# Gated MLP layer on one core: u and gate of 1088 tokens as seven products of halves, on quarters of 272 columns

## The chip, the core and the metric

The kernel runs on one core of a Trainium2 chip. Its metric is the device time of one execution in microseconds (us); three runs of the kernel before gave a median of 946.48 (944.19 to 948.4). The engines are TensorE (PE in the profile; PEld is its weight load), VectorE (DVE), ScalarE (ACT), GpSimd (POOL) and SyncE (SP), which issues all of the DMAs here. Each has its own queue of instructions.

## The reference

Two layers on 1088 tokens (1024 of a prompt, 64 of a sample), width 1024: a gated linear attention and a chunked MLP that mixes tokens, each with RMSNorm ahead and a residual; then a last RMSNorm. The change is in the second layer:

```python
def cmlp_mixer(h, w_in, ln_g, ln_b, w_spatial, b_spatial, w_out):
    u, v, gate = jnp.split(h @ w_in, 3, axis=-1)
    v = layernorm(v, ln_g, ln_b)
    ...
    mixed = jnp.einsum('gts,bnsgd->bntgd', ws, vg) + bs.T[:, :, None]
    z = u * mixed.reshape(bsz, t, CMLP_WIDTH) * jax.nn.silu(gate)
    return z @ w_out, v
```

## The kernel before

Activations lie in SBUF with 128 features on the partitions, 8 feature tiles `kt`, and tokens along the free axis. Tokens come in three pieces of 384, 384 and 320 (`PIECES`), each with an activation tile of its own (`act_slot`). Every float32 operand is split into a high and a low part in fp32r (ACT copies the high part, DVE subtracts it for the low part), and every product is three passes: high by high, high by low, low by high.

The second layer has three stages. The **v stage** (blocks 16 to 19 of the weights, nine chunks of 128 tokens each, the last 64) computes v by token and stores it to DRAM; beside it, `token_sums` builds sums of activations. The **u/gate loop** then goes over the eight column blocks `m` of 128. The **output products** (blocks 28 to 31) follow. From the v stage to the end of the loop every engine's instructions keep the order in which the code writes them (`in_order`).

In block `m`, u and gate of tokens 0 to 767 are one product of 2 x 2 quarters: the weights by (even or odd feature tile, u or gate), the activations by (even or odd feature tile, first or second 384 tokens). It takes seven products instead of eight (`product`, L987 to L990, 12 matmuls of 384 columns each). Four of them use sums of weight quarters, `s1` to `s4`; four use sums of activations, `tsum` 0 to 3. The sample and the rest of the prompt, 320 tokens, are done by plain products (`u` and `gate`, 24 matmuls of 320 columns each).

What sets the order of work in a block:

- `raw_quarters` (L937 to L940): SP loads the raw weights of a block, four DMAs of 256 KB, into one tile `rawq`. There is one such tile, so the next load waits for the last reader of the one before.
- `Quarters.sums` (L958, POOL): `s1` to `s4` from `rawq`. `Quarters.parts` and `plain` (`parts_of`, L943 to L946): high part on ACT, low part on DVE, of a sum or of a plain quarter such as (1,2).
- `v_load`, `v_norm`, `mixed` (L1062, L1072, L1088 to L1096): v of 128 columns comes from DRAM into `vm`, ACT normalizes it (nine steps), TensorE mixes it over tokens, DVE writes the result to `zt`. `v_out` (L1080, L1081, POOL) makes the output rows in `bc`.
- L1152 to L1154 and L1162 (POOL), L1141, L1161, L1169, L1170 (DVE): the seven products are joined into gate (`sg`) and u. `rs` is the norm's factor of each token. L1171 (ACT) is Silu, L1178 and L1184 (DVE) multiply the gate into `zt`, which is stored to DRAM. `pb`, `pe`, `p1` and `p6` are partial results; `pb` and `pe` are banks in PSUM that hold one product and then take another one on top.
- `late` (L1207 on) ends the plain part of a block inside the next block, and there issues the load of the weights for the block after that.

Of the kernel before, what the change touches and what calls it, by code (L numbers as in the profile page):

```python
# [28 lines left out]
NPMAX = 384  # L29

# [8 lines left out]
def trunk_kernel(ctx: ExitStack, tc: tile.TileContext, a: dict):  # L39
# [57 lines left out]
    rs = [cp.tile([P, n], F32, tag=f"rs{p}", name=f"rs{p}") for p, n in enumerate(size)]  # L97
# [88 lines left out]
    def act_slot(p, name):  # L186
        return ap_.tile([P, 2, KT, size[p]], F32R, tag=f"act{p}", name=name)
# [685 lines left out]
    kp = pool("sums23")  # L873
# [27 lines left out]
    tsum = [(kp if i in (1, 2) else mp).tile([P, 2, 4, NPMAX], F32R, tag=f"tsum{i}", name=f"tsum{i}") for i in range(4)]  # L901
# [6 lines left out]
    def split_to(dst, k, src):  # L908
        A.activation(dst[:, 0, k, :], src, AF.Copy)
        V.tensor_tensor(dst[:, 1, k, :], src, dst[:, 0, k, :].bitcast(F32), ALU.subtract)  # L910

    def token_sums(k):

        x = vp.tile([P, 2, 2, NPMAX], F32, tag="xsum", name="xsum")
        for p in range(2):
            SP.dma_start(x[:, p], a["x1_spill"][:, 2 * k:2 * k + 2, NPMAX * p:NPMAX * p + NPMAX])
# [32 lines left out]
    class Quarters:  # L949
        def __init__(self, blk):  # L950
# [3 lines left out]
            self.w = {}  # L954
# [19 lines left out]

    def quarter(p, e):
        return [(h1[p][:, 0, 2 * k + e, :], h1[p][:, 1, 2 * k + e, :]) for k in range(4)]

    class Halves:

        def __init__(self, *tiles):  # L980
            self.tiles = tiles

        def __getitem__(self, i):
            return self.tiles[i[2] // 4][i[0], i[1], i[2] % 4, i[3]]
# [9 lines left out]
    steps = (s for k in range(4) for s in token_sums(k))  # L994
    nxt = None
    for blk in range(16, 20):
        cs = slice((blk - 16) * 256, (blk - 15) * 256)
        for i in range(9):
            t = vp.tile([P, 256], F32, tag="vt", bufs=4, name="vt")
            if i < 8:  # L1000
                A.activation(t, tm_block(ws_[blk], h1[i // 3], (i % 3) * P), AF.Copy)  # L1001
# [8 lines left out]
            if blk < 19:  # L1010
                if i in (0, 1, 2):
                    load_w(blk + 1, i)
                if i in (2, 3, 4, 5):
                    fetch_w(blk + 1, [i - 2])
                    if i == 2:
                        load_w(blk + 1, 3)
            if (blk, i) == (16, 3):
                held.pop()(2)
            if blk == 17 and i in (2, 5, 8):
                token_rstd(i // 3)  # L1020
            if (blk, i) >= (16, 4):
                next(steps, None)
            if (blk, i) == (18, 4):
                nxt = Quarters(20)
            if blk == 19:
                if i == 0:
                    nxt.sums("s1")
                elif i == 1:
                    nxt.sums("s2")
                elif i == 2:  # L1030
                    nxt.sums("s3")
                    nxt.parts("s1")
                elif i == 3:
# [20 lines left out]
    nxt.plain((1, 1))  # L1054
# [5 lines left out]
    def v_load(m):  # L1060

        t = up.tile([P, 9, P], F32, tag="vm", bufs=2, name="vm")  # L1062
# [21 lines left out]
    def mixed(dst, vm, g, m, bias, c0, nch, sample):  # L1084

        pm = ps("o", "mix")
        for c in range(nch):
            PE.matmul(pm[:, c * P:(c + 1) * P], vm[:, c0 + c, :], ws[:, g, :], start=True, stop=True)  # L1088
        n = nch * P
        if sample:  # L1090
            PE.matmul(pm[:, n:n + NS], vm[:, 8, :], wss[:, g, :], start=True, stop=True)
        V.scalar_tensor_tensor(dst[:, :n].rearrange("p (c t) -> p c t", c=nch),
                               pm[:, :n].rearrange("p (c t) -> p c t", c=nch), lng[:, m:m + 1],
                               over(bias, nch), ALU.mult, ALU.add)
        if sample:
            V.scalar_tensor_tensor(dst[:, n:n + NS].rearrange("p (b t) -> p b t", b=NB),  # L1096
                                   pm[:, n:n + NS].rearrange("p (b t) -> p b t", b=NB), lng[:, m:m + 1],
                                   over(bias[:, :8], NB), ALU.mult, ALU.add)
# [273 lines left out]
```

## Time and profile before

| What | Value |
|---|---|
| Median of three runs | 946.48 us |
| The profiled execution, its own time | 945.69 us |
| Its span, first to last instruction | 943.9 us |
| Mean granted TensorE clock | 0.995 |
| Instructions | 16451 |
| HBM over the span | 103 GB/s |

The profile is of one execution. Busy time of an engine is the time in which an instruction of it runs; waits and DMA issues are not counted. Matmuls are pipelined, so one's duration overlaps the next. An idle time is put down to the instruction or transfer that ended last before it. Names such as L958 are lines of the kernel; `a<-b` reads "writes a, reads b".

### The profile page before, as it was taken

What the parts mean: (1) busy time and instruction counts of PE and PEld (TensorE: products, weight loads), DVE (VectorE), ACT (ScalarE), POOL (GpSimd) and SP (SyncE); (2) the same over time, 40 slices, a digit from 0 to 9 for tenths busy, and PEclk for the clock granted to TensorE, in tenths of its full rate; (3) what the DMA queues carried; (4) which work ended last, traced back from release to release, by engine and by line L of the source; (5) the groups of instructions that cost most, each with busy time, mean ns of one, the idle gap of its engine ahead of it and who ended that gap; (6) DMA issues with size and microseconds to landing.
All of it is one profiled execution on the core that took longest, in us unless ns stands there. A gap on an engine that the chain in (4) does not pass through costs nothing.

```text
span 943.9 us, 16451 instructions
## 1 busy us (share of the span) xinstructions
PE 909.9 (96%) x6149; PEld 884.2 (94%) x6149; DVE 624.3 (66%) x1239; ACT 447.0 (47%) x940; POOL 305.6 (32%) x315
## 2 busy tenths in 40 slices
PE   9989999999999999989999999999899999989995
PEld 8979989998999899978999999999899999989994
DVE  7888778677885877688552944455666666773246
ACT  7664544454462555464342733336444444454322
POOL 2023332333322331322143121144655555302123
PEclk9999999999999999999999999999999999999998
DMA  9302113311232112324574143523333333384233
GB/s 296 95 1 82 50 36 87 110 38 36 67 103 60 63 41 84 103 83 126 154 255 141 62 152 121 177 73 100 97 97 97 97 97 97 116 259 123 58 109 129
DMA packets 89644, 98.40 MB, mean 104 GB/s; under 512 B 9927, under 2 KB 82061, under 8 KB 89565
## 3 DMA queue, kind: packets, MB, share of 16 engines
q1 hardware_dynamic: 89564, 97.36, 33.6%
q8 instruction: 48, 0.79, 0.3%
q14 instruction: 32, 0.25, 0.1%
HBM read 70.92 MB, written 26.42 MB: 103 GB/s over the span
## 4 chain that ended last, share of the span: by engine, by line
PE 66%; DVE 15%; ACT 6%; issue 6%; DMA 5%; POOL 2%; SPq 1%; DVEq 0%; ACTq 0%; POOLq 0%
PE fm L132 26%; PE tm L146 15%; PE pb L990 4%; PE p L990 3%; PE pe L990 3%; PE u L990 2%; PE gate L990 2%; PE sc L508 2%; PE tms L162 1%; DVE wq L946 1%; PE pst L579 1%; PE mix L1088 1%; DMA xsum<-x_spill 1%; PE o L618 1%; DVE scT L521 1%
## 5 line engine op out<-in xcount | busy, mean ns | idle before, releaser
L146 PE MATMUL tm<-w,h 128*128 128x256 f32 (+1 forms) x1536 | 192.7, 283 | 1.6 <-ACT vt L1001 1.2
L132 PE MATMUL fm<-h,w 128*128 128x384 f32 (+1 forms) x1056 | 188.7, 333 | 0.1
L146 PEld LDWEIGHTS tm<-w,h 128*128 128x128 f32 x1536 | 185.4, 188 | 3.4 <-ACT vt L1001 1.6
L132 PEld LDWEIGHTS fm<-h,w 128*128 128x128 f32 x1056 | 174.4, 188 | 2.0 <-DVE h L196 0.7
L132 PE MATMUL fm<-og,w 128*128 128x384 f32 (+1 forms) x576 | 102.0, 332 | 0.4 <-DVE og L193 0.4
L132 PEld LDWEIGHTS fm<-og,w 128*128 128x128 f32 x576 | 95.1, 188 | 1.6 <-DVE og L193 0.6
L118 DVE TENSOR_TENSOR w<-wr,w 128x512 fp32r<-128x512 f32 (+1 forms) x96 | 71.3, 758 | 21.4 <-ACT w L117 20.6
L117 ACT ACTIVATE w<-wr 128x512 fp32r<-128x512 f32 (+1 forms) x96 | 58.6, 624 | 26.6 <-DMA wr<-w 14.5
L132 PE MATMUL fm<-zs,w 128*128 128x384 f32 (+1 forms) x384 | 64.0, 326 | 1.4 <-DVE x L838 1.4
L816 POOL TENSOR_TENSOR acc<-acc,sq 128x384 f32<-128x384 f32 (+1 forms) x30 | 30.9, 1034 | 105.6 <-ACT sq L811 105.1
L132 PEld LDWEIGHTS fm<-zs,w 128*128 128x128 f32 x384 | 62.3, 188 | 2.6 <-DVE x L838 2.0
L838 DVE TENSOR_TENSOR x<-fm,res 128x384 f32<-128x384 f32 (+1 forms) x40 | 21.0, 527 | 54.5 <-PE fm L132 54.5
L811 ACT ACTIVATE sq<-x 128x384 f32<-128x384 f32 (+1 forms) x42 | 21.0, 503 | 62.2 <-DVE x L838 59.4
L1008 DVE BATCH_NORM_STATS2 st<-vt 128x6 f32<-128x256 f32 (+1 forms) x36 | 15.2, 421 | 42.4 <-ACT vt L1001 42.2
L463 POOL TENSOR_TENSOR xe<-xe,k 128x384 f32<-128x384 f32 (+2 forms) x24 | 28.5, 1187 | 45.2 <-ACT xe L462 42.0
L649 POOL TENSOR_TENSOR on<-on,g 128x384 f32<-128x384 f32 (+1 forms) x24 | 23.8, 1013 | 57.0 <-DVE on L648 34.6
L439 POOL TENSOR_TENSOR kd<-kd,k 128x384 f32<-128x384 f32 (+1 forms) x12 | 12.0, 1004 | 85.8 <-ACT kd L438 85.8
L990 PE MATMUL pb<-tsum,wq 128*128 128x384 f32 x192 | 37.2, 341 | 2.5 <-DVE wq L946 1.4
L990 PEld LDWEIGHTS pb<-tsum,wq 128*128 128x128 f32 x192 | 33.7, 188 | 3.7 <-DVE wq L946 1.8
L990 PE MATMUL p<-h,wq 128*128 128x384 f32 x192 | 36.4, 337 | 0.0
L990 PE MATMUL pe<-tsum,wq 128*128 128x384 f32 x192 | 36.2, 336 | 0.0
L132 PE MATMUL fm<-tsum,w 128*128 128x384 f32 x192 | 34.3, 338 | 1.6 <-DVE z L1199 1.6
(271 smaller groups left out, 1855.2 us busy)
## 6 DMA issues: line engine op xcount, KB each, us to landing
wr<-w SPq DMA_DIRECT2D x92, 256.0 KB, 3.1
rawq<-w SPq DMA_DIRECT2D x32, 256.0 KB, 3.5
s<-s SPq DMA_DIRECT2D x16, 256.0 KB, 5.9
state_s<-ns SPq DMA_DIRECT2D x32, 128.0 KB, 2.5
v_spill<-vt SPq DMA_DIRECT2D x32, 128.0 KB, 1.8
vm<-v_spill SPq DMA_DIRECT2D x8, 512.0 KB, 4.3
xsum<-x_spill SPq DMA_DIRECT2D x8, 384.0 KB, 3.6
z_spill<-zt SPq DMA_DIRECT2D x16, 192.0 KB, 1.9
```

The source lines that it names most:

```text
L117: A.activation(w[:, 0], raw, AF.Copy)
L118: V.tensor_tensor(w[:, 1], raw, w[:, 0].bitcast(F32), ALU.subtract)
L132: PE.matmul(acc, lhs, rhs, start=(k == 0), stop=(k == 23))
L146: PE.matmul(acc, lhs, rhs, start=(k == 0), stop=(k == 23))
L463: G.tensor_tensor(xe, xe, kt_[:, :nl], ALU.mult)
L508: PE.matmul(bank[:, c, 0:192], xe[:, c * P:(c + 1) * P], xl[:, c * 192:(c + 1) * 192], start=True, stop=True)
L649: G.tensor_tensor(o, o, gate[h][:, j, t0:t0 + n], ALU.mult)
L811: A.activation(sq, raw[p][:, m, :], AF.Square)
L816: (V if gain is not None and p == 2 or m == KT - 1 else G).tensor_tensor(total, acc[p], sq, ALU.add)
L838: V.tensor_tensor(raw[p][:, m, :], pa, r, ALU.add)
L990: PE.matmul(acc, lhs, rhs, start=start and k + i == 0, stop=k + i == 5, skip_group_check=not start)
L1008: V.bn_stats(stats[i][:, blk - 16, :], t)
```

## The change

All 1088 tokens go into the seven products: the activations are now quartered by feature tile and by halves of 544 tokens, and each half is done as two quarters of 272 columns (`r` = 0, 1), since a PSUM bank holds 512. The plain products are gone, and with them `late` and the plain quarter (2,1). The three activation tiles become one, `act_all`; `act_slot` and `rs` are slices of it and of one `rs_all`. Three sums of activations are tiles of 544; the fourth (number 0) is written over the even feature tiles of the second half of `act_all`, once the v stage has read them, for which the last v block takes chunk 4 first. `vm`, `bias` have one buffer. In block 0 the order of the weight parts is one, in blocks 1 to 6 another.

```diff
+    rs_all = cp.tile([P, T], F32, tag="rs", name="rs")
+    act_all = ap_.tile([P, 2, KT, T], F32R, tag="act", name="act")
...
-    tsum = [(kp if i in (1, 2) else mp).tile([P, 2, 4, NPMAX], F32R, tag=f"tsum{i}", name=f"tsum{i}") for i in range(4)]
+    tsum = [None] + [mp.tile([P, 2, 4, HALF], F32R, tag=f"tsum{i}", name=f"tsum{i}") for i in (1, 2, 3)]
...
+    def token_sums(k, r):
+        x = vp.tile([P, 2, 2, QUART], F32, tag="xsum", name="xsum")
...
         G.tensor_tensor(b11, b12, b11, ALU.subtract)
-        G.tensor_tensor(b12, b22, b12, ALU.subtract)
+        V.tensor_tensor(b12, b22, b12, ALU.subtract)
+        V.tensor_tensor(b22, b22, b11, ALU.subtract)
+        V.tensor_tensor(b21, b21, b22, ALU.subtract)
...
+    def t1_sum(k):
+        x = first_x[k]
+        A.activation(x, x, AF.Copy, scale=ng[:, 1, 2 * k:2 * k + 1])
+        V.tensor_tensor(x[:, :HALF], x[:, HALF:], x[:, :HALF], ALU.subtract)
...
+        for j, i in enumerate((4, 5, 6, 7, 8, 0, 1, 2, 3) if blk == 19 else range(9)):
...
-        t = up.tile([P, 9, P], F32, tag="vm", bufs=2, name="vm")
+        t = up.tile([P, 9, P], F32, tag="vm", name="vm")
...
+        for r in R:
+            product(pb[r], w["s2"], tq[1][r])
+            A.activation(p6[r], pb[r], AF.Copy)
+            if first:
+                cur.parts("s4") if r == 0 else cur.plain((2, 2))
...
+        if more and not first:
+            for key in ("s1", "s2", "s3", "s4"):
+                nxt.sums(key, up if key == "s4" else None)
+        for r in R:
+            product(pe[r], w["s3"], tq[2][r])
+            A.activation(sg[:, qb[r]], pe[r], AF.Copy)
+            if first and r == 0:
+                cur.plain((1, 2))
+                nxt = Quarters(21)
+        v_norm(vm)
+        v_out(m, vm, bc)
+        for r in R:
+            product(pb[r], w["s1"], tq[0][r], start=False)
+            V.tensor_tensor(sg[:, qb[r]], sg[:, qb[r]], pb[r], ALU.add)
+        if more and not first:
+            nxt.parts("s2")
...
+        for r in R:
+            product(pa[r], w[1, 1], b11[r])
+            A.activation(p1[r], pa[r], AF.Copy)
+        for r in R:
+            G.tensor_tensor(p6[r], p6[r], p1[r], ALU.add)
+            G.tensor_tensor(sg[:, qb[r]], sg[:, qb[r]], p1[r], ALU.add)
+        for c in range(2):
+            mixed(zt, vm, g, m, bias, 4 * c)
+        V.tensor_tensor(sg[:, fb], sg[:, fb], rs_all[:, fb], ALU.mult)
+        if more and not first:
+            nxt.parts("s3")
+            nxt.parts("s1")
...
+        for r in R:
+            product(pb[r], w["s4"], b22[r], start=False)
+            V.tensor_tensor(p1[r], p1[r], pb[r], ALU.add)
...
+        mixed(zt, vm, g, m, bias, 0, True)
...
+            vm = v_load(m + 1)
+            if first:
+                for key in ("s1", "s2", "s3", "s4"):
+                    nxt.sums(key, up if key == "s4" else None)
+            else:
+                nxt.plain((1, 1))
+                nxt.parts("s4")
...
+        for r in R:
+            product(pe[r], w[2, 2], tq[3][r], start=False)
+            V.tensor_tensor(sg[:, qa[r]], p6[r], pe[r], ALU.add)
+        V.tensor_tensor(sg[:, fa], sg[:, fa], rs_all[:, fa], ALU.mult)
+        A.activation(sg, sg, AF.Silu)
+        if first:
+            for key in ("s2", "s3", "s1"):
+                nxt.parts(key)
+        elif more:
+            nxt.plain((2, 2))
+        else:
+            fetch_w(28, [0, 1])
...
+        G.tensor_tensor(sg[:, fb], sg[:, fb], rs_all[:, fb], ALU.mult)
+        V.tensor_tensor(sg[:, fa], sg[:, fa], rs_all[:, fa], ALU.mult)
+        for r in R:
+            product(pa[r], w[1, 2], b21[r], start=False)
+            V.tensor_tensor(zt[:, qa[r]], pa[r], zt[:, qa[r]], ALU.mult)
+        V.tensor_tensor(zt, zt, sg, ALU.mult)
+        SP.dma_start(z_d[:, m, :], zt)
+        if more:
+            if first:
+                nxt.plain((1, 1))
+                nxt.parts("s4")
+                nxt.plain((2, 2))
+            nxt.plain((1, 2))
+            if m + 2 < KT:
+                following = Quarters(22 + m)
```

POOL's queue in a middle block, before. Here `p` is a partial result, `qsum` and `qs` are the sums of weight quarters, and the row on `vm` closes the block:

```order
L1221 TENSOR_TENSOR sg_8334<-sg_8334,rs_81 128x320
L1080 TENSOR_TENSOR bc<-vm,bc 64x128
L1081 TENSOR_TENSOR bc<-bc 64x128
L1152 TENSOR_TENSOR p_8346<-p_8346,p_8347 128x384
L1153 TENSOR_TENSOR sg<-sg,p_8347 128x384
L1154 TENSOR_TENSOR sg<-sg,rs_80 128x384
L1162 TENSOR_TENSOR zt<-zt,p_8347 128x384
L958 TENSOR_TENSOR qsum<-rawq 128x512
L958 TENSOR_TENSOR qsum<-qsum,rawq 128x512
L1175 TENSOR_TENSOR sg<-sg,rs_80 128x384
L958 TENSOR_TENSOR qsum<-rawq 128x512
L958 TENSOR_TENSOR qs_8503<-rawq,qsum 128x512
```

The same engine and place after (`half` is a partial result of 272 columns):

```order
L977 TENSOR_TENSOR qsum<-rawq 128x512
L977 TENSOR_TENSOR qsum<-qsum,rawq 128x512
L977 TENSOR_TENSOR qsum<-rawq 128x512
L977 TENSOR_TENSOR qs_8311<-rawq,qsum 128x512
L1089 TENSOR_TENSOR bc<-vm,bc 64x128
L1090 TENSOR_TENSOR bc<-bc 64x128
L1161 TENSOR_TENSOR half<-half 128x272
L1162 TENSOR_TENSOR sg<-sg,half 128x272
L1161 TENSOR_TENSOR half<-half 128x272
L1162 TENSOR_TENSOR sg<-sg,half 128x272
L1177 TENSOR_TENSOR zt<-zt,half 128x272
```

The four sums of weights stood behind the adds on the activations; now they stand ahead of them.

DVE's queue from the end of one block to the start of the next, before. `wq` on the left is the low part of a weight operand:

```order
L1184 TENSOR_TENSOR zt<-zt,sg 128x768
L946 TENSOR_TENSOR wq<-qsum,wq 128x512 x3
L1199 TENSOR_TENSOR z_8731<-u,z_8731 128x320
L946 TENSOR_TENSOR wq<-qs_8743,wq 128x512
L946 TENSOR_TENSOR wq<-rawq,wq 128x512 x2
L1210 TENSOR_TENSOR sg_8814<-gate,rs_81 128x320
L946 TENSOR_TENSOR wq<-rawq,wq 128x512 x2
```

After, from the two adds behind the pass over `sg` that waits for POOL's adds (L1165) to the block's last step:

```order
L1176 TENSOR_TENSOR half<-half,pb 128x272 x2
L1099 TENSOR_TENSOR zt<-mix,lng,bias 128x64
L965 TENSOR_TENSOR wq<-rawq,wq 128x512
L965 TENSOR_TENSOR wq<-qs_8311,wq 128x512
L1195 TENSOR_TENSOR sg<-half,two 128x272 x2
L1196 TENSOR_TENSOR sg<-sg,rs 128x544
L965 TENSOR_TENSOR wq<-rawq,wq 128x512
L1207 TENSOR_TENSOR sg<-sg,rs 128x544
L1210 TENSOR_TENSOR zt<-p_8380,zt 128x272
L1210 TENSOR_TENSOR zt<-p_8381,zt 128x272
L1211 TENSOR_TENSOR zt<-zt,sg 128x1088
L965 TENSOR_TENSOR wq<-rawq,wq 128x512
```

The low parts of the weights stood together behind the block; now they stand between the passes of the block, and the last reader of `rawq` stands behind `zt<-zt,sg`.

More of the change, by code (lines that the diff above doesn't have):

```diff
@@ L29 @@
 NPMAX = 384
+HALF, QUART = 544, 272
 LOW = 16
@@ L1082, in v_out, with mixed @@
         SP.dma_start(a["v_out"][:, m * P:(m + 1) * P], bc[:, 2, :])
-    def mixed(dst, vm, g, m, bias, c0, nch, sample):
+    def mixed(dst, vm, g, m, bias, c0, sample=False):
         pm = ps("o", "mix")
[L1087 to L1098, printed above, removed]
@@ L1100, in trunk_kernel @@
-    zs = [None] * 3
+        gain = lng[:, m:m + 1]
+        if sample:
+            PE.matmul(pm[:, :NS], vm[:, 8, :], wss[:, g, :], start=True, stop=True)
+            V.scalar_tensor_tensor(dst[:, SEQ:].rearrange("p (b t) -> p b t", b=NB),
+                                   pm[:, :NS].rearrange("p (b t) -> p b t", b=NB), gain, over(bias[:, :8], NB),
+                                   ALU.mult, ALU.add)
+            return
+        for c in range(4):
+            PE.matmul(pm[:, c * P:(c + 1) * P], vm[:, c0 + c, :], ws[:, g, :], start=True, stop=True)
@@ L1160, in trunk_kernel @@
-        product(pb, w["s4"], b22, start=False)
-        V.tensor_tensor(p1, p1, pb, ALU.add)
-        G.tensor_tensor(zt[:, 1, :], zt[:, 1, :], p1, ALU.mult)
-        if not more:
-            for kt in range(3, 7):
-                split(zs[0], kt, nxt[:, kt, :] if kt < 5 else rest[kt - 5])
+        w, g, more = cur.w, m // 2, m + 1 < KT
+        first = m == 0
+        bias = up.tile([P, P], F32, tag="bias", name="bias")
+        zt = up.tile([P, T], F32, tag="zt", name="zt")
+        sg = up.tile([P, T], F32, tag="sg", name="sg")
@@ L1187, in trunk_kernel @@
-        if more:
-            nxt.sums("s3")
-            nxt.sums("s4", up)
-            for key in ("s2", "s1", "s3"):
-                nxt.parts(key)
-        else:
-            split(zs[0], 7, zt[:, 0, :])
-            fetch_w(28, [1, 2, 3])
-        u = ps("mm", "u")[:, :size[2]]
-        product(u, w[1, 1], quarter(2, 0))
-        product(u, w[1, 2], quarter(2, 1), start=False)
-        V.tensor_tensor(z2, u, z2, ALU.mult)
-        if more:
-            nxt.parts("s4")
-            nxt.plain((1, 1), (1, 2))
@@ L1203, in trunk_kernel @@
-        ga = ps("mm", "gate")[:, :size[2]]
-        product(ga, w[2, 1], quarter(2, 0))
-        product(ga, w[2, 2], quarter(2, 1), start=False)
-        s2 = tmp("hn", 2, size[2], "sg2")
-        def late(m=m, ga=ga, s2=s2, z2=z2, q=nxt if more else None):
-            nxt = None
-            V.tensor_tensor(s2, ga, rs[2], ALU.mult)
-            if q is not None:
-                q.plain((2, 2))
-            A.activation(s2, s2, AF.Silu)
-            if q is not None:
-                q.plain((2, 1))
-                if m + 2 < KT:
-                    nxt = Quarters(22 + m)
-                else:
-                    nxt = mp.tile([P, 5, N], F32, tag="rawq", name="zstage")
-                    SP.dma_start(nxt, z_d[:, 0:5, 0:N])
-            G.tensor_tensor(s2, s2, rs[2], ALU.mult)
-            V.tensor_tensor(z2, z2, s2, ALU.mult)
-            SP.dma_start(z_d[:, m, 2 * N:], z2)
-            return nxt
```

231 lines of the change are left out of this document (95 added, 136 removed).

## The prediction

> **What bounds the kernel now.** I read the page first. Its engine line has TensorE busy nearly all the time:
>
> ```profile
> PE 909.9 (96%) x6149; PEld 884.2 (94%) x6149; DVE 624.3 (66%) x1239; ACT 447.0 (47%) x940; POOL 305.6 (32%) x315
> ```
>
> Then the table by windows, cut at the first product of a block m of the u/gate loop (here m = 0, 1, 2 and 7; columns: window, its length, busy time of PE, PEld, DVE, ACT, POOL, granted clock, DMA share, GB/s):
>
> ```profile
> 637.00:661.19 24.19, 24.19 (x152) 23.95 (x151) 14.09 (x27) 15.26 (x34) 10.84 (x13) 1.00 0.35 97
> 661.19:688.05 26.86, 24.32 (x152) 23.67 (x151) 19.56 (x29) 12.79 (x27) 15.35 (x15) 1.00 0.40 114
> 688.05:711.84 23.79, 23.79 (x152) 23.79 (x151) 15.60 (x24) 10.64 (x22) 13.83 (x13) 1.00 0.31 97
> 806.99:832.52 25.53, 23.95 (x152) 23.71 (x151) 20.02 (x33) 8.90 (x18) 7.96 (x8) 1.00 0.42 127
> ```
>
> A steady block is bound by TensorE: 23.79 us, all busy, at full clock. The whole loop, 637.00 to 832.52, takes 195.5 us. Why the other engines keep up is in their order. POOL in a steady block, and what frees the raw weight tile `rawq` for its next load (DVE's low part of a plain quarter, then SP's four loads):
>
> ```profile
> 714.62 1.02 DVE L946 TENSOR_TENSOR wq<-rawq,wq 128x512 fp32r<-128x512 f32 x1 [0.46 <-ACT wq L945]
> 715.71 1.98 SPq L940 DMA_DIRECT2D rawq<-w  x4
> 721.02 1.01 POOL L1152 TENSOR_TENSOR p<-p,p 128x384 f32<-128x384 f32 x1 [4.40 <-ACT p L1144]
> 725.58 1.29 POOL L958 TENSOR_TENSOR qsum<-rawq 128x512 f32<-128x512 f32 x1
> 730.94 2.02 POOL L958 TENSOR_TENSOR qs<-rawq,qsum 128x512 f32<-128x512 f32 x1
> ```
>
> The loads go out at 715.71, and POOL asks for them only at 725.58, after its adds on the activations. The adds wait for TensorE alone (4.40 us idle before them), so the transfer hangs on nothing.
>
> **The change, part by part.**
>
> *The products.* Seven products of 12 matmuls at 384 columns and 48 plain ones at 320 become 168 at 272. TensorE's timeline of a steady block (start, duration; a piece's duration overlaps the next, so I use starts) and the group of 256-column matmuls:
>
> ```profile
> 699.90 2.28 PE L990 MATMUL pe<-tsum,wq 128*128 128x384 f32 x12
> 702.02 2.27 PE L990 MATMUL p<-h,wq 128*128 128x384 f32 x12
> 704.13 0.60 PE L1088 MATMUL mix<-ws,vm 128*128 128x128 f32 x4
> 704.72 3.77 PE L990 MATMUL u<-h,wq 128*128 128x320 f32 x24
> 708.32 3.68 PE L990 MATMUL gate<-h,wq 128*128 128x320 f32 x24
> 711.84 0.34 PE L990 MATMUL pb<-tsum,wq 128*128 128x384 f32 x1
> L146 PE MATMUL tm<-w,h 128*128 128x256 f32 x1344 | 165.7, 281 | 1.2 <-ACT vt L1001 1.2
> ```
>
> 384 columns cost 2.12/12 = 177 ns, 320 cost 7.12/48 = 148, 256 at most 165.7/1344 = 123. So 272 cost about 127 (123 to 137), and 168 of them 21.3 us, where the old ones take 84 x 177 + 48 x 148 = 22.0. The mixes stay (nine, regrouped; 23.79 - 22.0 = 1.8 us). A block needs 23.1 to 23.2 us of TensorE instead of 23.79: about 5 us over eight blocks, if TensorE stays the bound.
>
> *The order around them.* This decides. In blocks 1 to 6 three things now stand in one line. The load of `rawq` waits for DVE's low part of quarter (1,2), the last step of a block, behind `zt*sg`. POOL's four weight sums stand ahead of its adds on the activations, so a late load holds the adds up. And DVE waits for those adds at `sg*rs` of the second half, with everything up to the low part of (1,2) queued behind. That is a ring from load to load, closed without TensorE. If it is longer than 23.2 us, it sets the block. Its pieces come from block 0, where POOL did wait for the load, and from the ranges of single lines (ns min/median/max):
>
> ```profile
> 647.20 2.63 DVE L946 TENSOR_TENSOR wq<-rawq,wq 128x512 fp32r<-128x512 f32 x1 [2.73 <-ACT wq L945]
> 649.90 1.78 SPq L940 DMA_DIRECT2D rawq<-w  x4
> 646.35 0.45 POOL L1080 TENSOR_TENSOR bc<-vm,bc 64x128 f32<-64x128 f32 x1 [6.25 <-ACT vm L1072]
> 647.29 1.01 POOL L1152 TENSOR_TENSOR p<-p,p 128x384 f32<-128x384 f32 x1
> 648.25 1.02 POOL L1153 TENSOR_TENSOR sg<-sg,p 128x384 f32<-128x384 f32 x1
> 655.71 1.29 POOL L958 TENSOR_TENSOR qsum<-rawq 128x512 f32<-128x512 f32 x1 [3.28 <-DMA rawq<-w]
> 657.08 1.29 POOL L958 TENSOR_TENSOR qsum<-qsum,rawq 128x512 f32<-128x512 f32 x1
> 659.31 1.29 POOL L958 TENSOR_TENSOR qsum<-rawq 128x512 f32<-128x512 f32 x1
> 660.56 1.98 POOL L958 TENSOR_TENSOR qs<-rawq,qsum 128x512 f32<-128x512 f32 x1
> L946 DVE TENSOR_TENSOR wq<-rawq,wq x32: 671/678/2626, 640.4 to 809.8; 128x512 fp32r<-128x512 f32 x32
> L1169 DVE TENSOR_TENSOR sg<-p,pe 128x384 f32<-128x384 f32 x5 | 2.8, 555 | 7.3 <-PE pe L990 7.3
> L1096 DVE SCALAR_TENSOR_TENSOR z<-mix,lng,bias 128x64 f32<-128x64 f32 x5 | 1.3, 269 | 0.0
> L1178 DVE TENSOR_TENSOR sg<-sg,rs x8: 559/1243/1264, 655.1 to 825.5; 128x384 f32<-128x384 f32 x8
> L1184 DVE TENSOR_TENSOR zt<-zt,sg x8: 941/1460/2036, 659.4 to 828.0; 128x768 f32<-128x768 f32 x8
> L945 ACT ACTIVATE wq<-rawq x32: 613/616/624, 639.3 to 809.1; 128x512 fp32r<-128x512 f32 x32
> L1171 ACT ACTIVATE sg<-sg x8: 845/846/847, 654.2 to 824.6; 128x768 f32<-128x768 f32 x8
> L1171 ACT ACT_TABLE_LOAD   x1: 1283/1283/1283, 652.9 to 652.9; - x1
> ```
>
> From the end of the freeing step:
> 1. Load: DVE ends at 649.83, the first sum starts at 655.71, so 5.9 us. Now the store of `zt` (128 x 1088 x 4 bytes, 0.56 MB) goes out some 0.7 us ahead. I take 6.9 (5.9 to 8.0, below).
> 2. Four sums: starts 1.37 and 1.25 apart, the third again 1.25, the last 1.98: 5.9 us.
> 3. Two steps on `bc`: 646.35 to 647.29, 0.9.
> 4. Four adds of 272 columns on POOL. 384 take 0.96 from start to start; by columns 0.68, with a fixed part 0.71: 2.9.
> 5. DVE: one pass over 544 columns, two low parts, two adds of 272, the mix of 64 columns (0.27), two low parts, two adds, another 544. From 384 at 0.56 and 768 at 0.94 (the shortest of each row) come 0.45, 0.72 and 1.26 for 272, 544 and 1088; a low part is 0.67. Sum 6.2, less 0.08 overlap at nine joints, plus 0.2 for POOL's own steps beside it: 5.7.
> 6. ACT: Silu over 1088, 0.846 for 768 and so 1.2 by columns; the high part of (2,2) 0.62; with two handoffs 1.9.
> 7. DVE: low part, 544, two of 272, 1088, low part: 4.2, less overlap, plus POOL's `sg*rs` beside it: 4.3.
>
> With handoffs that is 28.7 us. All at the shortest it is 26.3; with DVE at its medians beside POOL, and the load at 8.0, about 31.5. Either way it is longer than TensorE's 23.2, so TensorE waits some 5.5 us a block: at the start of a block for `pb`'s bank (freed by DVE's `p1 + pb` of the block before, in step 5), and at the mixes.
>
> The 16 DMA engines under such loads:
>
> ```profile
> 652.00:653.00 1.00, 1.00 (x8) 1.00 (x7) 0.81 (x2) 0.08 (x1) 0.43 (x1) 1.00 1.00 289
> 654.00:655.00 1.00, 1.00 (x9) 1.00 (x9) 0.24 (x1) 0.99 (x2) 0.00 (x0) 1.00 0.69 257
> ```
>
> They are full at about 270 GB/s, so 0.56 MB ahead can cost between nothing and 2.1 us. The Trainium skill (DMA: Bandwidth & Descriptors, Issuing engines are not separate DMA queues) says that all DMAs run on the same 16 engines and interleave. By it the loads would wait out the rest of the store, 1.4 us, and the ring be 29.1 us.
>
> By block 0's row alone, with no store ahead, the ring would be 27.7 us. The store starts earlier and shares the engines, so I charge about half of the 2.1.
>
> *Block 0* is not in the ring: its sums come late, after its adds. TensorE runs through it (23.2 us). Behind its sixth pair of products, at about 20.8 us, DVE has 0.7, then the table load and Silu (2.5), three high parts (1.8, the last low part 1.2 behind them), 2.6 us of `sg` and `zt`, and four low parts (2.4): the load for block 2's weights goes out about 32 us after the loop's start, 9 into block 1. Block 1's first products, whose low part is ready at about 25.5, start some 2 us late, as today (26.86 against 23.79).
>
> *Block 7* follows six turns. ACT normalizes `vm`, in a row as this one:
>
> ```profile
> 642.70 3.57 ACT L1072 ACTIVATE vm<-vm,lt,lr 128x128 f32<-128x128 f32 x9
> 832.52 1.65 PE L132 MATMUL fm<-tsum,w 128*128 128x384 f32 x8 [1.58 <-DVE z L1199]
> ```
>
> By the durations above, from the last ring step: 3.6 for that row, POOL's `bc` and adds 3.8, DVE's 544 columns 0.7, seven low parts of `z` 3.6 (0.56 each, less overlap), two adds and the small mix 1.1, two adds and 544 columns 1.5, Silu 1.2, two low parts of output weights, 544 and two adds 2.5, `zt*sg` 1.2, and then two splits of `z` and two weight parts 2.5, under which TensorE does the first 12 of 24 matmuls. That is 21 us (19 to 23) to output products at full speed. The second row is today's end of the loop: 1.58 us of wait, since plain products covered DVE's tail; that cover is gone.
>
> The v stage before the loop, 561.5 to 637.0, in the same columns:
>
> ```profile
> sum 75.50, PE 74.29 PEld 73.65 DVE 36.44 ACT 27.93 POOL 21.38; mean PE 24.76 PEld 24.55 DVE 12.15 ACT 9.31 POOL 7.13
> ```
>
> *At nothing:* one tile for the activations (matmuls read the same columns, and each product's order before the loop is the same); sums 544 wide built there (on DVE 24 subtractions of 272, POOL's before, 10.8 us, four of 544, 2.9, and wider low parts, 4.7: 18 us more, where it is idle for 39); chunk 4 ahead of chunk 0 in the last v block; one `vm` buffer (its load goes out after the last mix and is asked for after two pairs of products). If the v stage's cover fails, I allow 2 us.
>
> *Sum:* 32 + 6 x 28.7 + 21 = 225 us against 195.5: +29.7. The profiled execution took 945.69 us (943.9 of span), 0.8 below the median of 946.48. So 945.7 + 29.7 + 0.8 = **976 us**.
>
> **The rivals.**
>
> *TensorE stays the bound.* If a ring turn is under 23.2 us, there are eight blocks of 23.2, some 2 us at block 1 and 3.5 at the end: 191 against 195.5, so 942 us, on the edge of faster. It decides from 5.5 us less than my sum: the load and the sums would have to be nearly halved. For it: POOL is busy 13.8 of 23.79 us, no engine is near full. Against it: each piece is a measured row in one enforced order. 7%.
>
> *A shorter ring*, 24 to 26 us a turn, if handoffs and the 272-wide steps overlap more than I think: 225 less 6 x 3.7 is 203, so 954 us. 5%. That 272 columns cost as much as 320 (148 ns) would make a block 24.9 + 1.8, still inside the ring: 976 again, and so no rival of its own.
>
> *POOL and DVE block each other.* Line L1178 takes 559 ns alone and 1243 in the median, with POOL running. If most two-input DVE steps of the ring paid such a wait, a turn would be 31.5 us: 993 us. The Trainium skill (SBUF — State Buffer, Who interferes with whom) says that a DVE instruction with two SBUF inputs and a GpSimd one that reads SBUF exclude each other for a whole instruction. This case's rows agree (559 against 1243). But in most of the ring POOL or DVE stands still, so I charge 0.6 us a turn. 8%.
>
> **How the numbers follow.** My forecast, turns of 26.3 to 31, holds 80%: 26.3 gives 32 + 158 + 20 = 210, so 961 us; 31 gives 239 or 240, so 991. Leaving out the fast rival, most of the short ring and the far end of the blocked one leaves out less than 20%: 957 to 992. What a measurement of this kernel can tell from no change is about 0.5%, or 4.7 us. The fast rival's 942 lies on that edge: faster 3%, same 5%, slower 92%.
>
> **What would show it.** Right: from block 2 on the starts of `pb` stand 28 to 30 us apart; TensorE idles before the first `pb` (released by DVE `half`) and before the mixes; POOL waits for the DMA of `rawq` before its first sum, DVE for POOL at `sg*rs`; a 272-column matmul starts every 127 ns. Wrong: `rawq` has landed before POOL asks for it, blocks of 23 us without gaps; or gaps of another cause, in the v stage or the output products.

## The result and the profile after

The changed kernel takes 1013.28 us (median of four runs, 1006.51 to 1015.26) against 945.6 us for the kernel before (four runs beside it): a ratio of 1.070 (95% interval 1.064 to 1.076). It is slower, as forecast, but by 67.7 us and not by 29.7. The profiled execution took 1014.11 us, its span is 1012.3 us.

The page's engine line and the chain of work that ended last. TensorE's share of the span falls from 96% to 92%, though it works longer:

```profile
PE 927.9 (92%) x6437; PEld 897.3 (89%) x6437; DVE 624.5 (62%) x1279; ACT 461.6 (46%) x972; POOL 283.6 (28%) x315
PE 46%; DVE 23%; DMA 9%; POOL 7%; issue 7%; ACT 6%; SPq 1%; DVEq 0%; POOLq 0%; ACTq 0%
```

In the chain TensorE has 46% where it had 66%; DVE, DMA and POOL have taken the rest. The chain of the kernel before:

```profile
PE 66%; DVE 15%; ACT 6%; issue 6%; DMA 5%; POOL 2%; SPq 1%; DVEq 0%; ACTq 0%; POOLq 0%
```

The table by windows, cut at the first product of each block (columns as in the prediction; here blocks 0, 1, 2 and 7, and the sum over all eight):

```profile
642.10:673.90 31.80, 26.08 (x189) 24.94 (x187) 13.18 (x31) 13.78 (x29) 11.86 (x15) 0.95 0.26 80
673.90:708.30 34.40, 28.00 (x186) 27.34 (x187) 17.47 (x28) 13.10 (x28) 12.46 (x15) 0.85 0.20 66
708.30:741.60 33.30, 25.71 (x189) 25.28 (x188) 15.23 (x24) 11.36 (x25) 13.48 (x15) 0.90 0.22 69
870.70:901.30 30.60, 25.29 (x189) 24.66 (x187) 16.67 (x30) 13.69 (x32) 6.98 (x9) 0.94 0.47 157
sum 259.20, PE 207.33 PEld 202.72 DVE 121.46 ACT 94.79 POOL 96.08; mean PE 25.92 PEld 25.34 DVE 15.18 ACT 11.85 POOL 12.01
```

A block takes 31 to 34 us where a steady one took 23.8. The loop takes 259.2 us against 195.5: 63.7 of the 68 us are here. No engine is full. TensorE stands still for 52 us of the loop, and it works for 207 us where eight blocks at full clock would be 185: the granted clock fell to 0.85 to 0.95.

TensorE's waits from the loop's start to its end (us in total, times, longest):

```profile
PE two L999 <- DVE sg L1195: 39.9, 8, 7.1
PE two L999 <- ACT sg L1145: 3.9, 8, 0.5
PE fm L137 <- DVE zt L1210: 2.5, 1, 2.5
PE pb L999 <- ACT wq L964: 2.4, 1, 2.4
PE pb L999 <- ACT rsum L1051: 2.3, 1, 2.3
PE pb L999 <- DVE wq L965: 0.9, 1, 0.9
```

The same list for the loop of the kernel before:

```profile
PE fm L132 <- DVE z L1199: 1.6, 1, 1.6
PE pb L990 <- DVE wq L946: 1.4, 1, 1.4
PE pb L990 <- ACT p L1125: 1.1, 1, 1.1
```

One wait carries 39.9 of the 52 us: TensorE waits at `two`, in the middle of a pair of products, for DVE's first reading of that tile. The prediction had it wait at `pb` and at the mixes; neither of these shows in a steady block. Block 2 on DVE's timeline (start, duration, what it is; in brackets the idle time before it and what ended that):

```profile
729.67 0.72 DVE L1165 TENSOR_TENSOR sg<-sg,rs 128x544 f32<-128x544 f32 x1 [3.68 <-POOL sg L1162]
...
734.42 0.42 DVE L1195 TENSOR_TENSOR sg<-half,two 128x272 f32<-128x272 f32 x1
738.02 0.44 DVE L1195 TENSOR_TENSOR sg<-half,two 128x272 f32<-128x272 f32 x1 [3.18 <-PE two L999]
738.50 0.72 DVE L1196 TENSOR_TENSOR sg<-sg,rs 128x544 f32<-128x544 f32 x1
740.98 1.51 DVE L965 TENSOR_TENSOR wq<-rawq,wq 128x512 fp32r<-128x512 f32 x1 [1.76 <-ACT wq L964]
...
745.14 0.69 DVE L965 TENSOR_TENSOR wq<-rawq,wq 128x512 fp32r<-128x512 f32 x1
```

And the same stretch on TensorE's:

```profile
726.05 1.75 PE L999 MATMUL two<-tsum,wq 128*128 128x272 f32 x12
734.90 3.09 PE L999 MATMUL two<-tsum,wq 128*128 128x272 f32 x12 [7.10 <-DVE sg L1195]
737.78 3.96 PE L999 MATMUL p<-act,wq 128*128 128x272 f32 x24
741.58 3.17 PE L999 MATMUL pb<-tsum,wq 128*128 128x272 f32 x24
```

`two` is one PSUM tile of two banks, and it holds both halves `pe[0]` and `pe[1]`. The first product ends at 727.8. The second writes the other bank, but the tile is one to whatever sets the waits: it waits until DVE has read the first, at 734.8. Then DVE waits 3.18 us for the second. So the product is a piece of the ring, and it runs at half clock: it takes 2.88 us from its start to the next product's, and the granted clock over these 2.88 us is 0.50. In a row without gaps 24 matmuls take 3.0 us, so twelve take 1.5.

The rest of this turn, first on POOL:

```profile
720.26 1.28 POOL L977 TENSOR_TENSOR qsum<-rawq 128x512 f32<-128x512 f32 x1 [10.85 <-DMA rawq<-w]
724.08 1.75 POOL L977 TENSOR_TENSOR qs<-rawq,qsum 128x512 f32<-128x512 f32 x1
725.79 0.45 POOL L1089 TENSOR_TENSOR bc<-vm,bc 64x128 f32<-64x128 f32 x1
726.73 0.76 POOL L1161 TENSOR_TENSOR half<-half 128x272 f32<-128x272 f32 x1
728.89 0.75 POOL L1162 TENSOR_TENSOR sg<-sg,half 128x272 f32<-128x272 f32 x1
```

The two loads that bound the turn, on SP, and between them Silu on ACT:

```profile
713.32 2.12 SPq L959 DMA_DIRECT2D rawq<-w  x4
...
739.31 1.11 ACT L1197 ACTIVATE sg<-sg 128x1088 f32<-128x1088 f32 x1 [12.82 <-DVE sg L1196]
...
745.85 2.11 SPq L959 DMA_DIRECT2D rawq<-w  x4
```

From load to load this turn is 32.5 us. POOL stands idle 10.85 us for the raw weights that the last step of the block before set free: the ring is there.

### The profile page after: what moved, and what is told of

It is laid out like the page before. It is cut to its first block, busy times and chain, and to the rows that moved or that the text cites. A ratio compares the mean times of both kernels' runs of the same rounds, so it can differ in the third digit from the quotient of the medians.

```text
span 1012.3 us, 17078 instructions
## 1 busy us (share of the span) xinstructions
PE 927.9 (92%) x6437; PEld 897.3 (89%) x6437; DVE 624.5 (62%) x1279; ACT 461.6 (46%) x972; POOL 283.6 (28%) x315
## 4 chain that ended last, share of the span: by engine, by line
PE 46%; DVE 23%; DMA 9%; POOL 7%; issue 7%; ACT 6%; SPq 1%; DVEq 0%; POOLq 0%; ACTq 0%
PE fm L137 23%; PE tm L151 10%; DVE wq L965 4%; PE two L999 3%; DMA rawq<-w 3%; DMA xsum<-x_spill 2%; POOL qsum L977 2%; DVE act L198 1%; PE sc L513 1%; POOL qs L977 1%; POOL half L1161 1%; POOL sg L1162 1%; PE o L623 1%; DVE scT L526 1%; DMA xt<-x_spill 1%
## 5 line engine op out<-in xcount | busy, mean ns | idle before, releaser
L137 PE MATMUL fm<-act,w 128*128 128x384 f32 (+1 forms) x2208 | 390.6, 333 | 3.7 <-DVE zt L1210 2.5
L137 PEld LDWEIGHTS fm<-act,w 128*128 128x128 f32 x2208 | 367.6, 189 | 7.9 <-issue 2.7
L151 PE MATMUL tm<-w,act 128*128 128x256 f32 (+1 forms) x1536 | 193.5, 283 | 3.2 <-ACT vt L1010 2.2
L151 PEld LDWEIGHTS tm<-w,act 128*128 128x128 f32 x1536 | 185.6, 188 | 5.5 <-ACT vt L1010 3.1
L999 PE MATMUL two<-tsum,wq 128*128 128x272 f32 x384 | 65.8, 329 | 43.8 <-DVE sg L1195 39.9
L999 PEld LDWEIGHTS two<-tsum,wq 128*128 128x128 f32 x384 | 59.5, 223 | 47.3 <-DVE sg L1195 41.6
L999 PE MATMUL p<-act,wq 128*128 128x272 f32 x384 | 55.1, 303 | 0.0
L999 PEld LDWEIGHTS p<-act,wq 128*128 128x128 f32 x384 | 54.2, 205 | 0.0
L999 PE MATMUL pb<-act,wq 128*128 128x272 f32 x384 | 51.4, 290 | 0.0
L999 PEld LDWEIGHTS pb<-act,wq 128*128 128x128 f32 x384 | 49.0, 189 | 0.0
L654 POOL TENSOR_TENSOR on<-on,g 128x384 f32<-128x384 f32 (+1 forms) x24 | 23.8, 1013 | 57.4 <-DVE on L653 34.7
```

What stands on the lines that cost most here:

```text
L137: PE.matmul(acc, lhs, rhs, start=(k == 0), stop=(k == 23))
L151: PE.matmul(acc, lhs, rhs, start=(k == 0), stop=(k == 23))
L654: G.tensor_tensor(o, o, gate[h][:, j, t0:t0 + n], ALU.mult)
L999: PE.matmul(acc, lhs, rhs, start=start and k + i == 0, stop=k + i == 5, skip_group_check=not start)
```

## The experiments

One theory and two rivals ran against each other first. **A**: the ring of the prediction sets blocks 1 to 6, and TensorE's second product of `two` is inside it. **B**: the gaps with their half clock cost the time by themselves. **C**: the order of POOL and DVE does, ring or no ring. Later rivals have letters of their own. Below, "turn" is the mean of five turns between the issues of `rawq`'s loads, "blocks" the mean of blocks 1 to 6 where nothing else is said. In the changed kernel the turn is 32.1 us (issues from 681.64 to 842.00) and the blocks 32.8.

**Both products of w(2,2) first.**

```diff
         for r in R:
             product(pe[r], w[2, 2], tq[3][r], start=False)
+        for r in R:
             V.tensor_tensor(sg[:, qa[r]], p6[r], pe[r], ALU.add)
```

> Both products of w(2,2) are issued ahead of the two DVE adds that read them; nothing else moves. Theory A (the ring of load, sums, POOL adds, DVE, Silu, low part of (1,2) sets blocks 1 to 6, and the second product of the tile `two`, which waits for DVE's first add, is inside it): DVE's wait of 3.2 us for that product goes, blocks 1 to 6 fall from 32.8 us in the mean to about 29.6, TensorE still has one gap of 5 to 7 us a block, the time falls by 6 x 3.2 = 19 to about 994 us. Rival B (TensorE's half clock after its gaps, not the ring, is what costs): the gaps stay, so the blocks stay within 1 us of 32.8 and the time within 6 us of 1013.

990.77 us, ratio to the kernel before 1.048 (1.045 to 1.052): 22.5 us less. The turn is 28.9 us and the blocks 28.8: the turn lost the 3.2 us that DVE had waited. In blocks 2 to 6 TensorE still idles 3 to 5 us a block (A had 5 to 7), and the clock is still 0.89 to 0.94. Blocks 3 and 4:

```profile
731.20:761.60 30.40, 25.82 (x188) 25.60 (x187) 16.46 (x27) 10.37 (x23) 13.74 (x16) 0.89 0.24 75
761.60:789.40 27.80, 24.93 (x189) 24.71 (x188) 12.58 (x21) 10.49 (x23) 11.64 (x13) 0.94 0.26 83
```

By B the blocks should have stayed, so B falls as the main cause; what the clock takes is measured further below. Two tiles for the two halves, the other way to part them, weren't tried.

**The sums behind the adds**, with all weight parts where block 0 has them, alone and together with the edit above:

```diff
-        if more and not first:
-            for key in ("s1", "s2", "s3", "s4"):
-                nxt.sums(key, up if key == "s4" else None)
...
         if more:
             vm = v_load(m + 1)
-            if first:
-                for key in ("s1", "s2", "s3", "s4"):
-                    nxt.sums(key, up if key == "s4" else None)
-            else:
-                nxt.plain((1, 1))
-                nxt.parts("s4")
+            for key in ("s1", "s2", "s3", "s4"):
+                nxt.sums(key, up if key == "s4" else None)
```

> In blocks 1 to 6 POOL's four weight sums and the weights' high and low parts stand where block 0 of the changed kernel has them: the sums behind POOL's product on zt, the parts of s2, s3, s1 behind Silu, the other four behind the store of zt. The tile `two` and everything else stays. Theory A: the ring is open, POOL no longer asks for the raw weights before its adds; blocks 1 to 6 are TensorE's 23.2 us and a wait of 1 to 3 us at the block's first product for the parts of s2, so about 25.5; block 7 about 27; the time about 965 us (955 to 980). Rival C (DVE and POOL side by side, more steps of 272 columns and the shared tile cost the time wherever the sums stand): blocks stay over 30 us, the time over 990.

> The edits of the two runs before together. Theory A: with the ring open the shared tile costs only the short wait of the second product for one DVE add, about 0.5 us a block, so 3 to 4 us less than with the sums late alone, about 962 us. Rival D (the shared tile costs as much with the ring open as inside it): some 19 us less than with the sums late alone.

981.84 us (ratio 1.039, 1.036 to 1.042) and 979.47 us (1.035, 1.032 to 1.038). The blocks are 27.3 and 26.8 us, 5.5 less than in the changed kernel, so the place of the sums matters; with them late the w(2,2) pair first saves only 2.4 us in all, near A's 3 to 4 and far from D's 19. (The s3 pair, not moved here, still made TensorE wait 7.3 us.) But both times lie some 17 us above A's: the blocks 2 us each, since TensorE waits for the parts of s2 at a block's first product and inside `two`, and block 7 most of all, 35.6 and 33.4 us where I had 27. C's 990 and more did not come either. The runs tell that the ring can be opened here, not yet what is left.

**The load left out.** `rawq` is not loaded again after block 0, so blocks 2 to 7 use the weights of block 1, and six loads of 1 MB (four of 256 KB each; the expectation has 0.5 MB) are left out. (A second tile for the raw weights, with the load kept, wasn't tried.)

```diff
-            self.rw = raw_quarters(blk)
+            self.rw = raw_quarters(blk) if blk < 22 else nxt.rw
```

> Leaves work out: blocks 2 to 7 take their weights from the raw tile that block 0 loaded for block 1, so six loads of 0.5 MB are gone, and POOL's sums at the start of blocks 1 to 6 wait for no load and for no low part of (1,2). The order of every engine is that of the changed kernel, the shared tile and the sums' place ahead of the adds too. Theory A: without the load the ring is open; blocks 1 to 6 come to TensorE's 23.2 us plus small waits, 23.5 to 25, the time about 958 us. Rival C (the order of POOL and DVE itself, the sums ahead of the adds, costs the time): POOL's adds still come 5.9 us of sums behind the block's start; blocks stay over 29 us, the time over 985.

980.73 us (1.035, 1.032 to 1.039). Blocks 2 to 6 take 26.4 us each, at a granted clock of 1.00, in the same order of instructions that took 32.5 with the load. C falls: POOL's sums ahead of its adds do no harm when they don't wait for a load. But A had 23.5 to 25. TensorE's timeline of one such block shows what is left:

```profile
759.78 1.67 PE L999 MATMUL two<-tsum,wq 128*128 128x272 f32 x12
762.97 1.77 PE L999 MATMUL two<-tsum,wq 128*128 128x272 f32 x12 [1.52 <-ACT sg L1145]
...
775.54 1.75 PE L999 MATMUL two<-tsum,wq 128*128 128x272 f32 x12
778.51 1.77 PE L999 MATMUL two<-tsum,wq 128*128 128x272 f32 x12 [1.21 <-DVE sg L1195]
```

Two waits, 1.52 and 1.21 us, both inside the shared tile, at each of its two pairs. 26.4 less 2.7 is 23.7. The next two runs take both away.

**Both pairs first**, alone and with the load left out:

```diff
         for r in R:
             product(pe[r], w["s3"], tq[2][r])
+        for r in R:
             A.activation(sg[:, qb[r]], pe[r], AF.Copy)
```

> Both pairs of products in the shared tile are issued ahead of the two steps that read them: the w(2,2) pair as in the run before with that edit alone, and now the s3 pair ahead of ACT's two copies too. Theory A (ring from load to load): with the first edit the products had left the ring; ACT's copies of the s3 pair and what follows (norm of vm, 6.3 us in all) run beside load and sums (11 us) and are not in it. So blocks 1 to 6 stay at 28 to 29 us (28.8 with the first edit alone), the time at 985 to 991. Rival E (TensorE's 25 us of waiting for those copies, seen in that run, is itself the cost): the blocks fall by 3 to 4 us, the time to about 970.

> Leaves work out: weights of blocks 2 to 7 from the raw tile loaded for block 1, no further load, as in the run with the load left out; and both pairs of products of the shared tile ahead of their readers. Theory A: with the ring open, all that held TensorE in a block of 26.4 us were the two waits inside the shared tile, 1.5 and 1.2 us; without them blocks 2 to 6 are 23.7 us, the time about 963 us (960 to 967). Rival F (the waits move to the next place, since DVE or ACT is as late as before): blocks stay over 25.5 us, the time over 975.

Alone: 987.02 us (1.043, 1.041 to 1.046), turn 28.3, blocks 28.1. This is the ring that the prediction worked out, closed without TensorE: 28.7 forecast, 28.3 measured. In the turn from 788.69 to 816.78 DVE waits for POOL (3.69 us at `sg*rs`) and for ACT (1.76), and not for TensorE. The waits at the copies of the s3 pair, 25 us in the run with the first edit, cost little, 4 us in all and 0.7 a block (E falls): TensorE now waits at the small mix instead (16.0 us in five waits, for DVE's reading of the mixes before it), because the ring sets the block. The list's first row, and one block's end on TensorE's timeline, where the two products stand together:

```profile
PE mix L1098 <- DVE zt L1105: 16.0, 5, 3.9
...
827.77 0.65 PE L1098 MATMUL mix<-wss,vm 128*128 128x64 f32 x2 [3.27 <-DVE zt L1105]
828.17 4.61 PE L999 MATMUL two<-tsum,wq 128*128 128x272 f32 x24
```

With the load left out: 957.55 us (1.011, 1.008 to 1.014), below the forecast 963 and its range; F falls. Its blocks 2 and 3:

```profile
696.60:719.70 23.10, 23.10 (x188) 23.10 (x188) 17.72 (x23) 10.35 (x24) 15.16 (x14) 1.00 0.17 54
719.70:742.80 23.10, 23.10 (x189) 23.10 (x188) 17.71 (x23) 10.36 (x24) 15.17 (x14) 1.00 0.16 53
```

TensorE is busy in all of 23.1 us. A steady block of the changed kernel, 32.5 us, is thus accounted for: 23.1 of TensorE, 3.3 for the shared tile without the load (26.4 less 23.1; 2.7 of it are the two waits), and the rest, some 6 us, the ring.

**The row sums early.** The product of the row sums and its copy `rsum` (3 lines) stand behind the first chunk of the last v block.

> The product of the row sums and its copy `rsum` stand behind the first chunk of the last v block instead of behind the last step on the activations; all else is the changed kernel. Theory A: in block 0 the wait of 2.3 us at the second product of s2 (for the bank that `rsum`'s copy frees, behind two late steps on the activations in ACT's queue) goes, and with it the half clock of the next 4 us; block 0 is 28 us instead of 31.7, nothing else changes, the time 1009 us. Rival G (the wait is only the first to be seen, ACT's queue is late anyway): the wait turns up at the shared tile's second product, block 0 stays over 30.5 us, the time at 1011 to 1015.

1014.17 us (1.071, 1.069 to 1.074): no difference. A falls here, and G was right. The wait of 2.3 us for `rsum` is gone, and TensorE waits 3.46 us at the shared tile's second product instead, behind the same late steps on the activations in ACT's queue:

```profile
647.07 1.97 PE L999 MATMUL two<-tsum,wq 128*128 128x272 f32 x12 [3.46 <-ACT sg L1146]
```

Block 0 is 31.7 us, as before the edit.

**The gap filled.** In blocks 1 to 6 the first product of w(2,2) is made four times over, which adds 27 us of work to TensorE.

```diff
             product(pe[r], w[2, 2], tq[3][r], start=False)
+            if r == 0 and more and not first:
+                for _ in range(3):
+                    product(pe[r], w[2, 2], tq[3][r], start=False)
```

> Adds work, and leaves the result wrong in these blocks: in blocks 1 to 6 of the changed kernel the first product of w(2,2) is made four times over, 3 x 1.5 = 4.5 us more of TensorE a block, in the gap of 5 to 7 us in which it waits for DVE. Theory A with the clock (the gap halves the granted clock, and the product behind it, at 2.9 to 3.1 us instead of 1.5, lies in the ring): the clock stays at 1.00, the product behind takes 1.5 us, a turn falls by about 1.4, six turns by 8, the time to about 1004 us (1001 to 1008) although TensorE does 27 us more. Rival I (the product is in the ring, but its length there comes from something else than the gap): the product behind still takes about 3 us, the time stays within 4 us of 1013 or rises.

1005.22 us (1.062, 1.060 to 1.064): 8 us less than the changed kernel, with more to do. The turn is 30.9 us, 1.2 less. In five of six blocks the product behind the gap now takes 1.6 us to the next product's start, in one, behind a gap of 2.06 us, 2.5; I falls. TensorE's timeline, with one of each:

```profile
692.20 6.27 PE L999 MATMUL two<-tsum,wq 128*128 128x272 f32 x48
699.71 1.76 PE L999 MATMUL two<-tsum,wq 128*128 128x272 f32 x12 [1.24 <-DVE sg L1198]
...
730.42 2.71 PE L999 MATMUL two<-tsum,wq 128*128 128x272 f32 x12 [2.06 <-DVE sg L1198]
```

So of what the product adds to a turn, about a third is the half clock (1.2 of 3.2 to 3.8 us), and the rest its work and the handoffs. It can be a little more, since the half clock still came once in six.

**The order repaired**, the whole computation, all products of 272 columns kept: both pairs first, `rsum` early, and

```diff
         for r in R:
             G.tensor_tensor(p6[r], p6[r], p1[r], ALU.add)
             G.tensor_tensor(sg[:, qb[r]], sg[:, qb[r]], p1[r], ALU.add)
+        if more:
+            nxt.sums("s1")
+            nxt.sums("s2")
...
         G.tensor_tensor(zt[:, qb[1]], zt[:, qb[1]], p1[1], ALU.mult)
         if more:
             vm = v_load(m + 1)
+            nxt.sums("s3")
+            nxt.sums("s4", up)
+            nxt.parts("s2")
```

the sums at the start of a block gone, the other parts behind Silu and behind the store, and in block 7 the load of `bc` ahead of `z`'s, the output weights' parts behind the last products on `zt`.

> Complete computation, the 272-column products kept. Both pairs ahead of their readers; POOL's sums s1 and s2 behind its adds on the activations, s3 and s4 behind its products on zt; the parts of s2 ahead of Silu, all others where block 0 has them; `rsum` early; in block 7 the load of bc ahead of the loads of z, and the parts of the output weights behind the last products on zt. Theory A: no ring, no wait in the shared tile, s2 ready in time: blocks 1 to 6 about 23.7 us, block 0 about 26, block 7 about 28; the time about 954 us (946 to 962). Rival H (without plain products at a block's end nothing covers Silu, the parts and zt*sg, so TensorE stops there whatever the order): blocks of 25.5 us and more, the time over 965.

955.27 us (1.010, 1.006 to 1.015), as forecast in sum, though not in its parts: blocks 0 and 1 take 23.2 us (I had 26 for block 0), blocks 2 to 6 25.6 to 26.1 (I had 23.7; H had 25.5 and more, so by the blocks H still stood). There TensorE waits for the parts of s3 and s2. POOL shows the cause:

```profile
760.91 0.45 POOL L1090 TENSOR_TENSOR bc<-vm,bc 64x128 f32<-64x128 f32 x1 [12.52 <-DMA bc<-lnbc]
```

The small load of `bc` was issued at 756.56, behind the four loads of raw weights, and landed at about 760.9; POOL's adds, sums and the parts behind them were late by that.

**`bc` ahead of the raw weights**, in the repaired kernel:

```diff
         if more:
...
+            bc = v_out_load(m + 1)
             if m + 2 < KT:
                 following = Quarters(22 + m)
```

> The repaired kernel of the run before, with the load of `bc` for the next block issued ahead of the loads of the raw weights instead of behind them. Theory A: in its steady blocks POOL stood idle for `bc` (12.5 us, until 4.3 us behind the load's issue), and its adds, the sums s1 and s2 and the parts behind them came 2.3 us later than TensorE's product on (1,1) allowed; without that TensorE's waits of 2.4 us a block for parts of the weights go, blocks 1 to 6 come to 23.2 us and the time falls by 5 x 2.4 = 12 to about 943 us (940 to 947), 0.3% under the kernel before. Rival H (Silu, the parts and zt*sg at the end of a block stop TensorE whatever the order): blocks stay at 25 us and more, the time at 952 or more.

943.3 us (median of 12 runs) against 946.13 (16 runs): a ratio of 0.998 (0.996 to 0.999). Its blocks 1 and 7, and the loop's sum:

```profile
663.60:686.70 23.10, 23.10 (x188) 23.10 (x187) 15.22 (x23) 10.71 (x24) 13.03 (x15) 1.00 0.32 99
802.30:826.70 24.40, 23.33 (x189) 23.14 (x187) 17.94 (x32) 14.23 (x32) 8.21 (x10) 1.00 0.51 158
sum 186.50, PE 185.39 PEld 184.98 DVE 124.07 ACT 89.30 POOL 93.86; mean PE 23.17 PEld 23.12 DVE 15.51 ACT 11.16 POOL 11.73
```

POOL no longer waits for `bc`: before its first step on it, at 743.41, it waits for ACT's normed `vm`. The loop takes 186.5 us, 9 less than in the kernel before and 73 less than in the changed one, with the same products. H falls: TensorE runs through the end of a block. So the order around the products of 272 columns made the loss, and not the products. This is the only version that beats the kernel before, and by 0.2% only, which is hardly more than no change: in its profiled execution 4.6 us of the loop's 9 are lost in the v stage (below) and 2 behind the loop.

## Why the prediction was right and wrong

**Right:** slower, by the ring from load to load. The 272-column matmul (24 of them start in 3.00 us, 653.43 to 656.43 in block 0, so 125 ns each; 127 forecast), TensorE's block of 23.1 to 23.2 us when nothing holds it, POOL's wait for the transfer, DVE's for POOL at `sg*rs`. And six of the ring's seven terms, in the turn from 713.32 to 745.85:

| Term | Forecast | Measured |
|---|---|---|
| 1 load, to the first sum | 6.9 | 6.9 |
| 2 four sums | 5.9 | 5.5 |
| 3 `bc` | 0.9 | 0.9 |
| 4 four adds | 2.9 | 2.9 |
| 5 DVE, `sg*rs` to `sg*rs` | 5.7 | 9.6 |
| 6 ACT, Silu and high part | 1.9 | 1.7 |
| 7 DVE, to the low part of (1,2) | 4.3 | 4.9 |
| sum, with handoffs | 28.7 | 32.5 |

(From the rows of this turn: 713.32, 720.26, 725.79, 726.73, 729.67 for `sg*rs`, 739.31 for Silu, 740.98 for the next low part, 745.85.)

That the ring without the product came so near, 28.3 against 28.7, is in part luck. In the turn from 788.69 to 816.78 of that run the load takes 5.7 us, 1.2 less than forecast, and terms 5 and 7 take 6.4 and 4.9, 1.3 more; these errors cancel. (In the six turns of the changed kernel the load takes 5.8 to 6.9 us. The 270 GB/s with which it was sized is a mean of two rows, and only the one with 289 has a full share.)

**Wrong: the step "a ring from load to load, closed without TensorE".** Term 5 counted two DVE adds side by side. Between them stands a product of TensorE: DVE's two adds start 3.60 us apart, and of that 3.18 is waiting. (The other 0.7 of the term's excess are small: POOL's products on `zt` beside two low parts.) Taking the product out gave back 3.2 to 3.8 us a turn (turn 28.9, then 28.3), and left the ring that the prediction had. The wait was in the code for the reading: `pe` is two slices of one tile `two`, and the pairs of products alternate with their readers. I looked at the tile as two banks. The same step named the wrong place: TensorE waits at `two`, near the end of a block, and when it gets to `pb` and the mixes of the next one, it doesn't wait there.

The clock follows from the same step. With TensorE outside the ring, its clock was of no account. In the ring it is: the gap of 5 to 7 us that the ring makes halves the clock of the one product that the ring then waits for, 1.2 us a turn.

**The sum, term by term.** The forecast for the loop was 32 + 6 x 28.7 + 21 = 225. The profiled execution has 39.4 (from 642.14 to the end of DVE's low part (1,2) at 681.6), 6 x 32.1 = 192.8 (to 874.4), and 26.9 (to 901.30): 7.4, 20.6 and 5.9 us over. Before the loop there are 5.1 us more, behind it 0.4 less; with them nearly all of the 38.7 us by which the profiled execution's 1014.1 passes the forecast for it, 945.7 + 29.7 = 975.4. The six turns, with 20.6 us, are over half of that.

- *"TensorE runs through" block 0*, 23.2 us and some 2 to the first product of block 1, took 31.7. It waits there for ACT, which stands behind two late steps on the activations, first at `rsum`'s bank, then in the shared tile; taking away the first alone changed nothing. In the repaired kernel, where both are gone and the sums of block 1 come sooner, block 0 takes 23.2. Which of these edits gave how much there wasn't separated. The traces show a part: where TensorE waits 1.1 us at `rsum`'s bank, block 0 takes 29.0 us as it is (the run with the sums behind the adds) and 27.0 with both pairs first alone; where it waits 2.3 to 2.4 us, 31.7 and 28.3 (both pairs first, the load left out). So both pairs first gives 2 to 3 us there, by single traces.
- *Block 7's 21 us* took 26.9: the norm of `vm` began 3.5 us after the last ring step and not at it, since ACT's second copy from `two` (877.64) waits for the second product; and DVE waits 2.72 us in the shared tile once more. Both are the same tile, read from the trace. It is not shown that the tile is the cause: with both pairs first these two waits are gone, and block 7, counted from its first product, takes 33.5 us against 30.6, since TensorE then waits 10.2 us for ACT's high part of `z`. The repaired order brought it down, to 24.4 us in the last run.
- *"At nothing" for the v stage* was wrong by more than the 2 us that I allowed: from its start to the first `pb` it takes 103.0 us in the changed kernel (539.15 to 642.14) and 100.4 before (536.61 to 637.01), and 102 to 106 in the experiments. TensorE waits there for ACT's copies of `vt` (2.2 us in the changed kernel, 3.5 in the last run), which stand behind the steps on the sums, and these behind late loads of `xsum` and `xt` (in the last run ACT stands idle 4.31 us for one of `xsum`). No run tried to mend that. The other 2.5 us before the loop lie ahead of the v stage, where nothing was changed; that point lies between 535.2 and 540.7 in the traces of these runs, so I take it for scatter.

**The rivals.** That TensorE stays the bound (942 us) is what the last repair shows, 943 us; the order decided against it. The price came out right partly by luck: the loop takes 186.5 us where the rival had 191, and the v stage, which it had at nothing, takes 4.6 us more. The rival of POOL and DVE blocking each other (a turn of 31.5) had nearly the turn that came, for another reason: POOL's and DVE's own terms came out as forecast to 0.7 us each, but for the product in term 5.

## What to carry to other kernels

Follow a ring by the tiles that the waits are set on, not by the banks or bytes that instructions touch: two halves in one tile, each written and read in turn, tie the writer to the reader of the other half. If one load buffer is freed by the last step of a block and asked for at the start of the next, add up the turn and compare it with the bound engine's block; opening it helped at each of the places tried here, but each waiting step that was hidden then shows, and a small load behind a big one is such a step. An edit that takes work from the bound engine at a block's end also takes the cover from what ran under it; here the order of the instructions could make up for that.

## What the runs showed of the hardware that was not expected

Gaps in TensorE's work cost twice. In the changed kernel each of the six gaps of 5.0 to 7.1 us before the second product of `two` was followed by twelve matmuls in 2.9 us instead of 1.6. With the gap filled to 1.2 to 2.4 us that came once in six, at 2.06 us, and not at 1.24, 1.81, 1.92, 2.08 and 2.38. So here all six long gaps brought the half clock, and among the short ones the length doesn't tell which did. The Trainium skill (TensorE: Matmul & The Clock Gate, Part 1: The HAM clock gate) says that the clock falls to half after an idle window of about 3.4 us, and that this window runs freely. The traces agree for the gaps of 5 us and more. They differ for the short ones: 2.06 us was enough once, as was 2.3 us in block 0 of the changed kernel (granted clock 0.57 over the 4 us from 647), and both are shorter than the page's window. The added matmuls, of no use to the result, made the kernel 8 us faster.
